# Layer 1 of a two-layer decoder step: squares summed by ScalarE, output halves added by Pool, weight casts on ScalarE

## The chip, the core and the metric

The kernel runs on one core of one Trainium2 chip. A core has five engines with their own instruction queues: TensorE (PE; its weight loads, PEld, overlap its matmuls), VectorE (DVE), ScalarE (ACT), GpSimd (POOL) and SyncE (SP), which here issues every DMA. Each queue runs in order: an instruction that waits holds up all behind it on its engine. The metric is the device time of one execution in microseconds (us), the median of several runs.

## What is computed

One inference step of a two-layer trunk: a prompt of 1024 tokens and 8 groups of 8 sample tokens (64 rows), width 1024. Layer 0 is gated linear attention, layer 1 stick-breaking attention with 16 heads of width 64; the change touches layer 1 alone, and the weight casts of its late part. Cut to layer 1, the reference is:

```python
hp = rms_norm(xp, norm_gain[1]);  u = hp @ w_in_b            # (1024 + 64) x 4096
q = rms_norm(u[..., :1024] by heads of 64, qnorm)
k = rms_norm(u[..., 1024:2048] by heads of 64, knorm)         # k and v are outputs too
v, g = u[..., 2048:3072], u[..., 3072:]
z = q.k / 8 + bias;  valid: key s < query t
rest = reverse cumsum of log(1 - sigmoid(z));  a = exp(z + rest)
x = x + ((a @ v) * silu(g)) @ w_out_b
```

`rms_norm` over a head is x * (mean(x*x) + 1e-6)^-0.5 * gain: for each token and each of its heads a sum of 64 squares.

## The kernel before

Matmuls take two fp32r parts of each operand (a high part and the rest), so each product is three matmuls. Layer 1 goes through 8 pairs of heads. For a pair `p`, `columns` computes q, k and v of each of 8 prompt tiles of 128 tokens and of the sample tile (24 matmuls of 384 columns, `dense`), `gates` the gate of each pair of tiles, and between them stand 20 units of attention, 128 x 512 logits each or a diagonal part of it: `logits` (PE, then two sigmoids `om` and `A` on ACT), `stick` (DVE scans), `turn` (PE transposes, ACT and DVE split the result into `aT`), `weigh` (PE into `po`).

After each tile of q, k, v stands `qk_sums` (L792 to L804): ACT squares the 128 x 256 of q and k from PSUM into `sq`, which has a 65th column per head with the constant 1e-6, and copies v out; DVE sums `sq` by heads into `ms` (L802); POOL raises to -0.5 into `rs` (L804). `qk_scale` (L810) multiplies on DVE from PSUM into `qk`; then the PSUM bank `acc` is free, of which there are two. For every two tiles `qk_p` transposes `qk` on PE and takes it apart with six ACT instructions (`qh` L853, `kc` L854 and L855) and four of DVE (`ql` L856 and L857, `kc` L858 and L859). `sq` has one buffer.

When a pair of heads has finished 256 tokens, `gate_b` joins the two heads: `po` holds the wanted halves on different partitions and columns, so for each half ACT copies one part to `sh` (L952) and DVE adds the other part from PSUM into `og` (L953); POOL multiplies by the gate (L954). This happens 32 times.

The weights are loaded in blocks of 128 x 512; `split` casts a block to the high part (`whi` or `w`), on ACT (L219) if it is used late (`e.first > ACT_FROM`) and `n % 8 < WHI`, else on DVE (L221); POOL subtracts for the low part (L222). Layer 1 from its third pair on, and the output projection, are late: of each 8 blocks 6 go to ACT and 2 to DVE.

Only PE's order is written out by hand, as due times that a heap sorts (`Timeline`, `at`). ACT, DVE, POOL and SP get their order from the framework's own planner. The framework keeps ACT and DVE apart where both would read the same partitions of one PSUM bank.

Of the kernel before, what the change touches and what calls it, by code (L numbers as in the profile page):

```python
# [9 lines left out]
F32 = mybir.dt.float32  # L10
# [3 lines left out]
AF = mybir.ActivationFunctionType  # L14
OP = mybir.AluOpType
AX = mybir.AxisListType
# [11 lines left out]
SH, DH = 16, 64  # L28
# [3 lines left out]
EPS = 1e-6  # L32
# [4 lines left out]
def cut(base, offset, ap):  # L37
    return bass.AP(tensor=base.tensor, offset=base.offset + offset, ap=ap)
# [38 lines left out]
def tile_hybrid_decoder(ctx, tc, x_prompt, x_sample, state_gla, cache_k, cache_v, page_table,  # L77
# [3 lines left out]
    nc = tc.nc  # L81
# [12 lines left out]


    FIRST0, FIRST, FIRST5, RAW0 = 0.9, 1.5, 6, 0.9
    ACT_FROM, WHI, DLO = 90, 6, 3

    GAIN, CONSTS, SUP, LATE = -64.9, 2.5, 0.9, 9
    LAT, LAT0, LQ, LK = .7, 1.2, 1.4, 1.3  # L100
# [18 lines left out]
    def opened(name, side="left", **how):  # L119
        cm = tc.tile_pool(name=name, bufs=2, side=side, reuse_waits="tile", **how)  # L120
        pools[name] = cm.__enter__()
        pools[name, "cm"] = cm
# [5 lines left out]
    def sb(pool, name, shape, dtype=F32, bufs=2, tag=None):  # L128
        return pools[pool].tile(shape, dtype, name=name, tag=tag or name, bufs=bufs)
# [4 lines left out]
    def rows(t):  # L134
        return 128 if t < NP else NS
# [22 lines left out]
    def bcast(dst, src, off, n):  # L158
        nc.sync.dma_start(dst, cut(src, off, [[0, 128], [1, n]]))
# [87 lines left out]
    def rsqrt(dst, mean):  # L247
        nc.gpsimd.tensor_scalar(mean, mean, EPS, None, op0=OP.add)
        nc.gpsimd.tensor_tensor(dst, mean, half_exp[:mean.shape[0], :mean.shape[1]], op=OP.pow)
# [83 lines left out]
    def whole_rows(st, pool, n=512):  # L333
        up = sb(pool, "xr", [128, 512], F32, NX[pool])
        nc.scalar.activation(up[:64, :n], st["ps"][64:128, :n], AF.Copy)
        nc.vector.tensor_add(up[:64, :n], st["ps"][:64, :n], up[:64, :n])
        st["ps"] = up
# [4 lines left out]
    half_exp = const.tile([128, 4], F32, name="half_exp")  # L342
# [73 lines left out]
    for t in range(NP + 1):  # L416
        st = {}
# [14 lines left out]
    for c, (c_0, n) in enumerate(CH):  # L432
        st = {}
# [228 lines left out]
    for h in range(GH):  # L662
# [3 lines left out]
        for c, (c_0, n) in enumerate(CH):  # L666
            st = {}
# [11 lines left out]
            for j, (key, out) in enumerate((("q", q_out), ("k", k_out))):  # L679
                lo, hi = a + (b - a) * 0.5 * j, a + (b - a) * 0.5 * (j + 1)  # L680
                dense_t(lo, hi, c_0, n, wqk,
                        lambda w, k, j=j: (w[k // 2], slice((k % 2) * 256 + j * 128, (k % 2) * 256 + j * 128 + 128)),
# [4 lines left out]
        for t in range(NP + 1):  # L687
            st = {}
# [50 lines left out]
    for c in range(2):  # L739
        w = weights([load_cols(w_out_a, D, k, c * 512, 0, 1, 512) for k in range(NK)])  # L740
        for t in range(NP + 1):
            st = {}
# [24 lines left out]
    K1 = {}  # L767

    def l1_consts():
        opened("keep")  # L770
        opened("at1")
        qn = K1["qn"] = const.tile([128, 1], F32, name="qn")
        for j in range(2):
            nc.sync.dma_start(qn[j * 64:(j + 1) * 64], cut(qnorm_b, 0, [[1, 64], [1, 1]]))
        nc.vector.tensor_scalar(qn, qn, DH ** -0.5, None, op0=OP.mult)
        bcast(K1.setdefault("kn", const.tile([128, DH], F32, name="kn")), knorm_b, 0, DH)
        knt = K1["knt"] = const.tile([128, 1], F32, name="knt")
        for j in range(2):
            nc.sync.dma_start(knt[j * 64:(j + 1) * 64], cut(knorm_b, 0, [[1, 64], [1, 1]]))
        bias = K1["bias"] = const.tile([128, 2, SH], F32, name="bias")  # L780
        bcast(bias[:, 0], sb_bias, 0, SH)
        nc.vector.tensor_scalar(bias[:, 1], bias[:, 0], -1.0, None, op0=OP.mult)
        gains = K1["gains"] = const.tile([128, 1], F32, name="gains")
        nc.vector.tensor_mul(gains, qn, knt)
        for name in ("qTs", "kTs", "gTs"):
            K1[name] = sb("keep", name, [128, PAIRS, NS], F32, 1)

        K1["sq"] = sb("at1", "sq", [128, 4, DH + 1], F32, 1)
        nc.gpsimd.memset(K1["sq"][:, :, DH:], EPS)

    def qk_sums(st, p, t):
        n = rows(t)  # L792
        if t == NP:
            whole_rows(st, "at1", 384)
        ps = st["ps"]
        sq = K1["sq"]
        q4 = ps[:n, :256].rearrange("p (h d) -> p h d", d=DH)
        ms = small.tile([128, 4], F32, name="ms4")
        nc.scalar.activation(sq[:n, :, :DH], q4, AF.Square, scale=1.0 / 8.0)  # L799
        st["v"] = sb("at1", "v", [128, 128])  # L800
        nc.scalar.activation(st["v"][:n], ps[:n, 256:384], AF.Copy)
        nc.vector.tensor_reduce(ms[:n], sq[:n], axis=AX.X, op=OP.add)  # L802
        st["rs"] = small.tile([128, 4], F32, name="rs4")
        nc.gpsimd.tensor_tensor(st["rs"][:n], ms[:n], half_exp[:n], op=OP.pow)  # L804

    def qk_scale(st, p, t):
        n, ps, rs = rows(t), st["ps"], st["rs"]
# [138 lines left out]
    def gate_b(q, pair, p, m):  # L946
        po = q["po"]
        sh, og = sb("at2", "sh", [128, 256], F32, 1), sb("at2", "og", [128, 256], F32, 2)
        q["og"] = og
        for j in range(2):  # L950
            main, other = slice(64 * j, 64 * j + 64), slice(64 - 64 * j, 128 - 64 * j)
            nc.scalar.activation(sh[main], po[other, j], AF.Copy)  # L952
            nc.vector.tensor_add(og[main], po[main, j], sh[main])  # L953
        nc.gpsimd.tensor_mul(og, og, pair["g"][m])  # L954

    def tps(m):
# [13 lines left out]
    def take_h(st, m, g, n):  # L970
        ks = slice(2 * g, 2 * g + n)
        nc.scalar.activation(H[0][:, ks, tps(m)], st[g], AF.Copy)
        nc.vector.tensor_sub(H[1][:, ks, tps(m)], st[g], H[0][:, ks, tps(m)])

    at(i + 0.7, l1_consts)

    def open_at2():
# [12 lines left out]
    for p in range(PAIRS):  # L990
# [4 lines left out]
        def columns(t, i, span):  # L995
            st = {}
            dense(i, t, w, st, span, 384)
            e = i + span
            at(e + 0.02, qk_sums, st, p, t)
            at(e + C_SC, qk_scale, st, p, t)  # L1000
            sts.append(st)
            if t < NP:
                at(max(e + C_SC, open2), v_parts, st, t, pair)
            if t == NP:
                at(e + C_TS, qk_s, st, p)
            elif t % 2 == 1:
                at(max(e + C_T, open2 + 0.01 * t), qk_p, sts[t - 1:], pair)
            at(max(e + C_T, open2) + 0.2, kv_store, st, p, t)
            return e
# [8 lines left out]
        for m in range(NP // 2):  # L1018
            i = columns(2 * m, i, 0.75)
            i = columns(2 * m + 1, i, 0.75)  # L1020
            ready = max(i + UNIT0, open2 + 0.5)
            if m < NP // 2 - 1:
                i = gates(m, i, 0.5)
            else:
                i = gates(m, i, 0.625)
                i = columns(NP, i, 0.5)
            q = {}
            units = [(j, c) for j in range(2) for c in range(m, -1, -1)]
            for x, (j, c) in enumerate(units):
                u = {}  # L1030
                z0 = max(free, ready)
                free = z0 + PACE
                at(z0, logits, u, pair, p, m, c, j)
                at(z0 + L_STICK, stick, u, pair, m, c, j)
                at(z0 + L_TURN, turn, u, m, c)
                at(z0 + L_AV, weigh, u, q, pair, m, c, j, x == 0, x == len(units) - 1)
            at(z0 + L_AV + 0.05, gate_b, q, pair, p, m)
            at(z0 + L_AV + 0.35, store_b, q, p, m)
            if p == PAIRS - 1:
                st = {}  # L1040
                for g in range(4):
                    n = 2 if g < 3 else 1
                    at(i + 0.1 + 0.05 * g, load_h, st, m, g, n)
                    at(i + 0.6 + 0.05 * g, take_h, st, m, g, n)
# [161 lines left out]
    for c, t in steps[:2 * NP - TAIL] + [(0, NP), (1, NP)] + steps[2 * NP - TAIL:]:  # L1206
        if t == NP and c == 0:
            i = max(i, s1 + S_GAP)
        st = {}
# [44 lines left out]
```

## Time and profile before

| | |
|---|---|
| median of 3 runs | 1348.04 us (1348.0 to 1350.47) |
| the profiled execution | 1349.09 us, its span 1347.4 us |
| PE busy | 1269.9 us (94%) |
| DVE busy | 1011.1 us (75%) |
| ACT busy | 708.4 us (53%) |
| POOL busy | 515.5 us (38%) |

The shares are means over the whole span; layer 0, layer 1 and the last projection have different limits. Layer 1's loop over pairs runs from about 524 to 1232 us of the span. A busy PE is not one at its peak: a matmul's listed duration overlaps that of the next. The granted TensorE clock is full throughout.

### The profile page before, as it was taken

To read this page: it belongs to the slowest core of one execution; us is meant where nothing else is said; L and a number is where in the kernel's file an instruction comes from. 1 tells how busy PE (TensorE), PEld (TensorE's weight loads), DVE (VectorE), ACT (ScalarE), POOL (GpSimd) and SP (SyncE) were. 2 spreads that over 40 slices of the span, in tenths; PEclk is the share of its full clock that TensorE was granted. 3 is DMA by queue.
4 is the path that set the end of the run, shared out by engine and by line. 5 is a ranking of instruction groups with operands and counts; after the bars stand their busy time and mean duration, and the time that the engine had idled before them with its cause. 6 is when DMAs were issued, how large, how long until landed. Compare 5 with 4: busy or idle time off the path is not lost.

```text
span 1347.4 us, 23358 instructions
## 1 busy us (share of the span) xinstructions
PE 1269.9 (94%) x8025; PEld 1128.5 (84%) x8025; DVE 1011.1 (75%) x2047; ACT 708.4 (53%) x1640; POOL 515.5 (38%) x847
## 2 busy tenths in 40 slices
PE   6899999999999999989989999899998999999998
PEld 5788888888887787889989899898898998978665
DVE  7857858759565357698898988988889889896543
ACT  6446245254352034566666766667667677763221
POOL 6222323223222215363453734646446464443000
PEclk9999999999999999999999999999999999999999
DMA  6311402403327443020120200202002022134862
GB/s 193 91 41 44 135 20 59 124 17 100 121 90 240 135 137 117 20 73 27 34 71 23 71 27 28 79 23 70 28 28 77 21 78 86 33 124 152 316 204 79
DMA packets 118456, 115.80 MB, mean 86 GB/s; under 512 B 11002, under 2 KB 97922, under 8 KB 118338
## 3 DMA queue, kind: packets, MB, share of 16 engines
q1 hardware_dynamic: 118338, 114.31, 27.5%
q8 instruction: 64, 1.05, 0.3%
q14 instruction: 54, 0.44, 0.1%
HBM read 83.61 MB, written 30.67 MB: 85 GB/s over the span
## 4 chain that ended last, share of the span: by engine, by line
PE 56%; DVE 25%; ACT 7%; issue 5%; POOL 4%; DMA 3%; SPq 0%; DVEq 0%; POOLq 0%; ACTq 0%
PE acc L293 33%; PE acc L315 6%; DVE run L907 4%; PE z L881 3%; PE tr L928 3%; PE o L942 2%; DVE aT L931 2%; DVE whi L221 2%; ACT qh L853 2%; DVE qk L810 1%; POOL rs L804 1%; DVE A L912 1%; DVE A L915 1%; PE o L544 1%; DVE run L904 1%
## 5 line engine op out<-in xcount | busy, mean ns | idle before, releaser
L293 PE MATMUL acc<-whi,h 128*128 128x512 f32 (+1 forms) x1728 | 538.1, 374 | 9.3 <-DVE qk L810 6.2
L293 PEld LDWEIGHTS acc<-whi,h 128*128 128x128 f32 x1728 | 312.8, 189 | 40.3 <-ACT sh L952 3.8
L293 PE MATMUL acc<-wlo,h 128*128 128x512 f32 (+1 forms) x864 | 322.6, 373 | 3.9 <-DVE wlo L222 2.5
L315 PE MATMUL acc<-h,whi 128*128 128x256 f32 (+5 forms) x832 | 191.7, 316 | 19.1 <-DVE qk L810 8.7
L222 POOL TENSOR_TENSOR wlo<-wr,whi 128x512 fp32r<-128x512 f32 x98 | 144.4, 1478 | 127.4 <-DVE whi L221 92.5
L293 PEld LDWEIGHTS acc<-wlo,h 128*128 128x128 f32 x864 | 162.5, 188 | 22.1 <-DVE wlo L222 3.2
L315 PEld LDWEIGHTS acc<-h,whi 128*128 128x128 f32 (+2 forms) x832 | 137.8, 185 | 26.2 <-issue 10.6
L907 DVE TENSOR_TENSOR_SCAN run<-om,run 128x256 f32<-128x256 f32 x192 | 141.8, 779 | 15.6 <-ACT om L884 15.1
L930 ACT ACTIVATE aT<-tr 128x512 fp32r<-128x512 f32 (+1 forms) x160 | 89.0, 556 | 82.8 <-PE tr L928 80.9
L884 ACT ACTIVATE om<-z,bias 128x512 f32<-128x512 f32 (+1 forms) x160 | 103.1, 644 | 48.3 <-PE z L881 39.6
L293 PE MATMUL acc<-w,h 128*128 128x384 f32 (+1 forms) x480 | 122.0, 365 | 0.8 <-DVE qk L810 0.8
L315 PE MATMUL acc<-h,wlo 128*128 128x256 f32 (+2 forms) x392 | 122.2, 312 | 0.3 <-POOL wlo L222 0.3
L931 DVE TENSOR_TENSOR aT<-tr,aT 128x512 fp32r<-128x512 f32 (+1 forms) x160 | 100.9, 631 | 9.7 <-ACT aT L930 7.4
L928 PE MATMUL tr<-ident,A 128*128 128x128 f32 x576 | 90.0, 274 | 18.6 <-DVE kc L859 8.4
L885 ACT ACTIVATE A<-z,bias 128x512 f32<-128x512 f32 (+1 forms) x160 | 102.4, 640 | 0.0
L942 PE MATMUL o<-aT,v 128*128 128x256 f32 (+1 forms) x640 | 98.1, 274 | 0.0
L928 PEld LDWEIGHTS tr<-ident,A 128*128 128x128 f32 x576 | 68.9, 140 | 34.0 <-ACT sq L799 9.0
L942 PEld LDWEIGHTS o<-aT,v 128*128 128x128 f32 x640 | 94.4, 188 | 1.7 <-DVE aT L931 1.0
L804 POOL TENSOR_TENSOR rs<-ms,half_exp 128x4 f32<-128x4 f32 (+1 forms) x72 | 86.2, 1198 | 21.3 <-DVE ms L802 18.8
L881 PE MATMUL z<-kc,qh 128*128 128x256 f32 x320 | 84.4, 286 | 7.2 <-DVE kc L858 7.2
L293 PEld LDWEIGHTS acc<-w,h 128*128 128x128 f32 x480 | 83.2, 189 | 6.3 <-issue 0.8
L899 POOL COPY run<-run 128x2 f32<-128x2 f32 x96 | 32.8, 342 | 135.7 <-DVE run L907 78.1
(273 smaller groups left out, 2488.7 us busy)
## 6 DMA issues: line engine op xcount, KB each, us to landing
wr<-in_w_in_b_dram SPq DMA_DIRECT2D x64, 256.0 KB, 3.0
wr<-in_w_in_a_dram SPq DMA_DIRECT2D x32, 256.0 KB, 2.9
kp<-in_cache_k_dram SPq DMA_DIRECT2D x16, 512.0 KB, 4.6
vp<-in_cache_v_dram SPq DMA_DIRECT2D x16, 512.0 KB, 4.9
o_d<-og SPq DMA_DIRECT2D x60, 128.0 KB, 1.8
x<-in_x_prompt_dram SPq DMA_DIRECT2D x8, 512.0 KB, 5.2
wr<-in_w_in_a_dram SPq DMA_DIRECT2D x32, 128.0 KB, 3.9
n<-in_state_gla_dram SPq DMA_DIRECT2D x8, 512.0 KB, 4.2
```

Of the source, the lines that this page charges most:

```text
L222: engine.tensor_sub(e.lo[:, :m], raw[:, :m], e.hi[:, :m])
L293: nc.tensor.matmul(st["ps"][:x.shape[1], :n], x, (w[k].hi if part == 0 else w[k].lo)[:, :n], start=first, stop=last)
L315: nc.tensor.matmul(st[key][:x.shape[1], :n], x, y, start=first, stop=last)
L804: nc.gpsimd.tensor_tensor(st["rs"][:n], ms[:n], half_exp[:n], op=OP.pow)
L881: nc.tensor.matmul(out, lhs, rhs, start=x == 0, stop=x == len(mm) - 1)
L884: nc.scalar.activation(u["om"][:, v0:], z[:, v0:], AF.Sigmoid, scale=-1.0, bias=K1["bias"][:, 1, hd:hd + 1])
L885: nc.scalar.activation(u["A"][:, v0:], z[:, v0:], AF.Sigmoid, bias=K1["bias"][:, 0, hd:hd + 1])
L907: nc.vector.tensor_tensor_scan(run[:, a, n - 1::-1], rev, rev, before[:, a, 0:1], op0=OP.mult, op1=OP.bypass)
L928: nc.tensor.transpose(tr[:, x], u["A"][:, col:col + 128], ident)
L930: nc.scalar.activation(hi[:, v0:], tr[:, v0:], AF.Copy)
L931: nc.vector.tensor_sub(lo[:, v0:], tr[:, v0:], hi[:, v0:])
L942: nc.tensor.matmul(q["po"][:, j, q0:], vs, part[:, x * 256 + q0:(x + 1) * 256], start=first and n == 0, stop=last and n == 3)
```

## The change

Three edits, all in layer 1 but for four blocks of the output projection's weights:

- `qk_sums`: in place of one square over 256 columns, four squares over 64 columns each, every one of which also writes its sum by ScalarE's accumulator; the sum on DVE and the constant column go, and POOL adds 1e-6 ahead of the power (`rsqrt`, two POOL instructions in place of one).
- `gate_b`: ACT copies both parts of each half (four copies in place of two), and one add on POOL over 128 x 256 takes the place of two adds on DVE over 64 x 256.
- `WHI` from 6 to 8: every late weight cast is on ACT.

```diff
-    ACT_FROM, WHI, DLO = 90, 6, 3
+    ACT_FROM, WHI, DLO = 90, 8, 3
...
-        K1["sq"] = sb("at1", "sq", [128, 4, DH + 1], F32, 1)
-        nc.gpsimd.memset(K1["sq"][:, :, DH:], EPS)
+        K1["sq"] = sb("at1", "sq", [128, 4, DH], F32, 1)
...
-        nc.scalar.activation(sq[:n, :, :DH], q4, AF.Square, scale=1.0 / 8.0)
+        for h in range(4):
+            nc.scalar.activation(sq[:n, h], q4[:, h], AF.Square, scale=1.0 / 8.0, accum_out=ms[:n, h:h + 1])
         st["v"] = sb("at1", "v", [128, 128])
         nc.scalar.activation(st["v"][:n], ps[:n, 256:384], AF.Copy)
-        nc.vector.tensor_reduce(ms[:n], sq[:n], axis=AX.X, op=OP.add)
         st["rs"] = small.tile([128, 4], F32, name="rs4")
-        nc.gpsimd.tensor_tensor(st["rs"][:n], ms[:n], half_exp[:n], op=OP.pow)
+        rsqrt(st["rs"][:n], ms[:n])
...
             main, other = slice(64 * j, 64 * j + 64), slice(64 - 64 * j, 128 - 64 * j)
+            nc.scalar.activation(og[main], po[main, j], AF.Copy)
             nc.scalar.activation(sh[main], po[other, j], AF.Copy)
-            nc.vector.tensor_add(og[main], po[main, j], sh[main])
+        nc.gpsimd.tensor_add(og, og, sh)
         nc.gpsimd.tensor_mul(og, og, pair["g"][m])
```

`rsqrt`, which layer 0 already uses (L248, L249), is:

```python
    def rsqrt(dst, mean):
        nc.gpsimd.tensor_scalar(mean, mean, EPS, None, op0=OP.add)
        nc.gpsimd.tensor_tensor(dst, mean, half_exp[:mean.shape[0], :mean.shape[1]], op=OP.pow)
```

## Rows read from the trace of the kernel before

**Rows 1.** Busy time by stretch: start:end, length, then each engine's busy us (instructions).

```profile
524.00:1232.00 708.00, 662.36 (x4550) 627.82 (x4549) 605.44 (x1159) 468.85 (x996) 351.53 (x595) 1.00 0.18 53
752.00:776.00 24.00, 20.77 (x139) 19.08 (x138) 23.58 (x38) 17.45 (x37) 20.43 (x23) 1.00 0.32 92
```

**Rows 2.** The page's chain that ended last, whole span, by engine.

```profile
PE 56%; DVE 25%; ACT 7%; issue 5%; POOL 4%; DMA 3%; SPq 0%; DVEq 0%; POOLq 0%; ACTq 0%
```

**Rows 3.** PE's waits, 524 to 1232 us: total us, times, longest.

```profile
PE acc L315 <- DVE qk L810: 10.4, 7, 1.7
PE tr L928 <- DVE kc L859: 8.4, 6, 2.4
PE z L881 <- DVE kc L858: 7.2, 10, 1.4
PE acc L293 <- DVE qk L810: 7.0, 14, 1.2
PE tr L928 <- ACT sq L799: 4.5, 7, 1.0
```

**Rows 4.** ACT's waits, 524 to 1232 us, same columns.

```profile
ACT qh L853 <- PE tr L829: 19.9, 24, 2.6
ACT sq L799 <- DVE ms L802: 6.6, 7, 1.3
```

**Rows 5.** Timelines of ACT, DVE, POOL, PE around one tile: start, us, engine, line, tiles.

```profile
773.57 0.38 ACT L799 ACTIVATE sq<-acc 128x256 f32<-128x256 f32 x1 [0.74 <-PE acc L293]
...
777.74 0.42 DVE L802 TENSOR_REDUCE ms<-sq 128x4 f32<-128x260 f32 x1
...
778.24 1.01 POOL L804 TENSOR_TENSOR rs<-ms,half_exp 128x4 f32<-128x4 f32 x1
...
779.28 0.42 DVE L810 TENSOR_TENSOR qk<-acc,rs 128x256 f32<-128x256 f32 x1 [0.66 <-POOL rs L804]
...
779.85 0.41 PE L293 MATMUL acc<-w,h 128*128 128x384 f32 x1 [0.24 <-DVE qk L810]
```

**Rows 6.** Groups by line (L221: 590 to 1260 us): count, busy us, mean ns, idle before.

```profile
L802 DVE TENSOR_REDUCE ms<-sq 128x4 f32<-128x260 f32 (+1 forms) x72 | 29.1, 405 | 0.9 <-ACT sq L799 0.9
L953 DVE TENSOR_TENSOR og<-o,sh 64x256 f32<-64x256 f32 x64 | 26.6, 415 | 2.8 <-ACT sh L952 1.1
L221 DVE CAST whi<-wr 128x512 fp32r<-128x512 f32 x11 | 7.6, 693 | 0.0
L221 DVE CAST w<-wr 128x512 fp32r<-128x512 f32 x5 | 3.2, 631 | 2.0 <-DMA wr<-in_w_out_b_dram 2.0
```

**Rows 7.** ACT's timeline in layer 0: a square with accumulator, and what follows it.

```profile
202.59 0.39 ACT L645 ACTIVATE og<-o 128x256 f32<-128x256 f32 x1
202.87 0.20 ACT L645 ACTIVATION_READ_ACCUMULATOR og<-o 128x1 f32 x1
202.96 0.38 ACT L529 ACTIVATE gt<-acc 128x256 f32<-128x256 f32 x1
```

**Rows 8.** Groups by line, 524 to 1232 us: nearest rows of the added work.

```profile
L866 ACT ACTIVATE gTs<-acc 128x64 f32<-128x64 f32 x8 | 1.7, 218 | 0.0
L952 ACT ACTIVATE sh<-o 64x256 f32<-64x256 f32 x64 | 24.3, 379 | 39.5 <-DVE og L953 35.4 <-PE o L942 3.1
L219 ACT ACTIVATE whi<-wr 128x512 fp32r<-128x512 f32 x36 | 22.4, 631 | 6.0 <-DMA wr<-in_w_in_b_dram 5.6 <-DMA wr<-in_w_out_b_dram 0.3
L954 POOL TENSOR_TENSOR og<-og,gt 128x256 f32<-128x256 f32 x32 | 26.6, 830 | 37.9 <-DVE og L953 37.9
```

**Rows 9.** Line L248, layer 0's add ahead of the power: ns min/median/max.

```profile
L248 POOL TENSOR_SCALAR ms<-ms x36: 216/224/557, 75.7 to 417.1; 128x1 f32<-128x1 f32 x32, 64x1 f32<-64x1 f32 x4
```

**Rows 10.** DVE's timeline: the same two scans beside POOL's L954 and without it.

```profile
752.51 1.83 DVE L907 TENSOR_TENSOR_SCAN run<-om,run 128x256 f32<-128x256 f32 x2
...
775.62 1.38 DVE L907 TENSOR_TENSOR_SCAN run<-om,run 128x256 f32<-128x256 f32 x2
```

**Rows 11.** POOL's timeline beside the first of them.

```profile
752.56 1.24 POOL L954 TENSOR_TENSOR og<-og,gt 128x256 f32<-128x256 f32 x1
```

## The prediction

> **What bounds the kernel now.** I read the busy times by stretch first, because the shares of the whole span mix layers and the change touches layer 1 alone. There [rows 1] PE is busy 662 of 708 us, DVE 605 (86%), ACT 469 (66%), POOL 352 (50%). So PE comes first and DVE is close behind it; over the middle 24 us of one pair of heads DVE is busy for 23.6, while PE falls to 20.8 and ACT to 17.5. In that stretch DVE sets the pace, in the rest of the pair PE does. The chain that ended last says the same of the whole span [rows 2]: PE 56%, DVE 25%, ACT 7%, POOL 4%. What can be won is therefore PE's idle time in layer 1, and the next view is who ends it [rows 3]. Two families hold most of it: PE waits for a bank of `acc`, which `qk` on DVE sets free (10.4 + 7.0 = 17.4 us), and for `kc` on DVE, the end of a burst of six ACT and four DVE instructions after the transposes of `qk` (8.4 + 7.2 = 15.6 us, 16 waits); 4.5 us are marked with the square on ACT, that is, with how far ACT's queue has come. The last view is ACT's own waits, because ACT receives the work: it stands 35.4 us before the second `sh`, held by DVE's first add [rows 8], and 6.6 us before the square, held by the sum in the single `sq` [rows 4]. During these 42 us nothing behind gets out of ACT's queue.
>
> **What DVE loses.** 72 sums of 0.405 us (29.1 us), 64 adds (26.6 us) and the 16 casts still on DVE from the third pair on (7.6 + 3.2 = 10.8 us) [rows 6]: 66.5 of its 605 us. Little of DVE's work is left over as idle time, so nearly all of it moves DVE's queue forward; on PE's waits only a part shows.
>
> **What ACT gains.** No row of layer 1 shows an accumulating square, but layer 0 has one [rows 7]: the square runs 0.39 us, the read of the accumulator starts 0.28 us after it, and the next instruction 0.09 us after that. So a read costs a slot of 0.09 us and a square gives up its slot about 0.11 us before its listed end. The nearest 64-column instruction from PSUM lasts 0.218 us [rows 8], a slot of 0.11. Four heads take 4 x (0.11 + 0.09) = 0.80 us against 0.28 now: +0.52 us, by 72 tiles +37 us. The other end is that nothing overlaps: 4 x (0.218 + 0.20) = 1.67 against 0.39, +1.28 us a tile, +92 us. I take the first, since the overlap is read from the very pair of instructions; the second is a rival. The 64 further copies are like `sh`, 0.379 us listed, 0.28 as slots: +18 us (at most 24). The casts are 16 x 0.63 us = 10 us [rows 8]. Together +65 us (at most +126). Against it the 42 us of standing still fall away: `sq` is no longer read by anybody, and the copies of `po` need no DVE between them. ACT is thus bound for 469 + 65 = 534 us (75%), at most 595 (84%).
>
> The Trainium skill ("ScalarE: Activation LUTs", What ACT_TABLE_LOAD costs) gives 186 ns plus 0.833 ns an element for such an instruction, and 93 ns of overlap back to back. That would make 64 columns 239 ns, where the row has 218; as an estimate from the page four squares would take 4 x 146 = 584 ns of slots, without the reads, for which it has no price.
>
> **What POOL gains.** 72 adds of 1e-6, 0.224 us for one column [rows 9] and hardly more for four: 16 us; no lower than zero, no higher than 0.3 us each, since the instruction is nearly all fixed cost. And 32 adds over 128 x 256 like the multiply beside them, 0.830 us [rows 8]: 27 us. POOL goes from 352 to 395 us (56%). Both stand in chains: the first between the squares and `rs`, the second ahead of the gate multiply, which only a store waits for. Behind them in POOL's queue stand the copies of `run`, for which DVE's multiply waits, and the low parts of weights.
>
> POOL's add also takes something from DVE. Two scans that take 1.38 us alone took 1.83 us beside POOL's multiply of the same shape, which itself took 1.24 us [rows 10, 11]. Thirty-two adds cost DVE 32 x 0.45 = 14 us by that; nothing if they fall beside other work, 32 x 1.24 = 40 us if DVE stood still throughout. I take 14 us, from the row of the same shape. Net DVE loses 66.5 - 14 = 52 us.
>
> **The sum, on PE's waits.**
> 1. The `acc` bank, 17.4 us. In the tile shown [rows 5] the square ended at 773.95, DVE came to the sum at 777.74, `rs` ran to 779.25 and `qk` followed. After the change the squares would end by 774.5, the add and the power by 776, and `qk` could follow the scans two us earlier. Elsewhere the way is one of 0.5 us through DVE, which the longer squares and the added POOL instruction give back. I take half: -9 us, with ends of -17 and 0.
> 2. The burst before `kc`, 15.6 us. ACT's part begins after a wait for PE's transposes 24 times in 32 [rows 4], and there nothing in front of it matters. The other 8 may have a set of squares in front: 8 x 0.52 = +4 us, ends -3 (DVE comes earlier to its part) and 8 x 1.28 = +10.
> 3. What is left of DVE's relief, 26.6 + 10.8 - 14 = 23 us, shortens the end only where DVE is on the chain, 25% [rows 2]: -6 us, ends -23 and 0.
> 4. ACT's net load, 65 - 42 = +23 us, at its 7% of the chain [rows 2]: +2 us, ends -4 (the waits marked with the square) and +6 (84 x 7%).
>
> Together -9 us. From the profiled execution's 1349.1 us (span 1347.4 and 1.7 around it) that is 1340; the median lies 1 us lower, so 1339 us. Layer 0 and the last projection keep their work but for four casts.
>
> **Rivals.**
> *No change.* PE's order is fixed by hand and the power on POOL stays in the chain; if `rs` then ends the same waits a little later (add 0.22 us, squares 0.52 us, against a sum of 0.42 us taken out), steps 1 and 3 give nothing that step 2 doesn't take: 1348 us. For it: `qk` already waited for `rs` in the tile shown [rows 5]. Against it: the 3.8 us before the sum there.
>
> *Slower, ACT ends last.* The accumulator lets nothing overlap, a set of squares holds ACT for 1.67 us, and in the sigmoids' and `aT`'s way. ACT then is bound for 84% of layer 1, as DVE is now. Of the 72 sets a third, about what DVE and ACT hold of the chain together [rows 2], stands in front of something that PE waits for: 24 x 1.28 = +31 us. The same third of the 42 us of standing still is won, -14 us; steps 1 and 3 give nothing, since ACT is late instead of DVE: 1348 + 31 - 14 = 1365 us. It decides from the point where a set costs more than the standing still that it ends, 42 us / 72 = 0.58 us a tile; my 0.52 is close below, and that is the weakest point of the forecast.
>
> *Slower, Pool's port.* If DVE stands still through POOL's whole add, 40 us are lost against the 26.6 saved, and the gate's chain is an instruction longer. At 25% to 50% on the chain that is +3 to +7 us, with step 1 lost 1352 to 1356. The Trainium skill says so ("GPSIMD Engine Reference", Engine selection): elementwise work with two inputs belongs on VectorE, GpSimd being about twice as slow. By the rows the engine time is a draw here: one add of 0.830 us [rows 8] for two of 0.415 over half the partitions each [rows 6].
>
> **How the numbers follow.** Forecast (1322 to 1345) 50%, no change 17%, ACT last 22%, Pool's port 11%. This kernel's measurement can tell about 0.2%, 2.7 us, from no change. So faster 0.50, same 0.17, slower 0.33. Cases of both signs are open, so the range goes from 1322 (steps 1 and 3 near their ends, -26 us) to 1364, just short of the whole of the ACT rival: that leaves out some 15 of the 22% and the far end of the forecast.
>
> **What would show it.** In the profile after: an ACT line of 288 short squares and as many reads, and the start of one to the next tells 0.20 us from 0.42; PE's waits for `qk` down from 17.4 to under 10 us; ACT's waits for `og` and `ms` gone; DVE's busy time in layer 1 at 540 to 555 us. PE's waits for `kc` above 26 us, or ACT above 80% in layer 1, would speak for the ACT rival; scans longer on the mean than now, for the Pool rival. The forecast is wrong if the planner puts the four squares in front of the sigmoids.

## The result, and the profile after

The changed kernel takes 1363.69 us (median of 4 runs, 1361.17 to 1364.02), the kernel before 1348.02 in the same session: a ratio of 1.0106, 95% interval [1.0093, 1.0119]. It is slower by 1.1%, where 1339 us was forecast. The result lies inside the stated range only because its end of 1364 was set by the rival with ACT, which didn't come true (below). The profiled execution took 1361.17 us, with a span of 1358.7.

The busy times of layer 1 in the kernel after, columns as in [rows 1]:

```profile
524.00:1232.00 708.00, 657.64 (x4494) 623.70 (x4493) 567.95 (x1004) 529.70 (x1572) 400.94 (x697) 1.00 0.17 52
```

The engine loads came out near the forecast: DVE 568 us (forecast 553), ACT 530 (534), POOL 401 (395). PE, the engine that matters, did 5 us less work in the same stretch than before [rows 1]. Who it waited for (total us, times, longest; compare [rows 3]):

```profile
PE acc L315 <- DVE qk L808: 18.8, 8, 2.9
PE acc L293 <- DVE qk L808: 7.9, 14, 1.2
PE z L879 <- ACT sq L798: 4.7, 8, 0.9
PE tr L926 <- ACT sq L798: 4.0, 7, 0.6
PE tr L926 <- DVE A L913: 3.9, 7, 1.0
```

The waits for `kc`, 15.6 us before, have all but gone (3.2 us in all, below these rows). The waits for `qk` went from 17.4 to 26.7 us. ACT's own longest waits name neither `og` nor `ms` any more, so what was to fall away there did:

```profile
ACT aT L928 <- PE tr L926: 71.2, 71, 3.4
ACT om L882 <- PE z L879: 35.9, 70, 2.0
ACT qh L851 <- PE tr L827: 24.1, 18, 6.1
```

And the squares overlap as forecast. ACT's timeline around one set:

```profile
775.05 0.22 ACT L798 ACTIVATE sq<-acc 128x64 f32<-128x64 f32 x1
775.16 0.21 ACT L798 ACTIVATION_READ_ACCUMULATOR sq<-acc 128x1 f32 x1
775.25 0.28 ACT L800 ACTIVATE v<-acc 128x128 f32<-128x128 f32 x1
```

The four squares of this set start at 774.47, 774.66, 774.86 and 775.05 and `v` follows at 775.25: 0.195 us a head with its read, 0.78 us a set, where 0.80 was forecast and 1.67 was the rival's.

So what was slow? Follow the set just shown through POOL, DVE and PE. It belongs to the first tile of a pair of heads (POOL's, DVE's and PE's rows in turn):

```profile
775.97 1.28 POOL L222 TENSOR_TENSOR wlo<-wr,whi 128x512 fp32r<-128x512 f32 x1
777.33 0.29 POOL L248 TENSOR_SCALAR ms<-ms 128x4 f32<-128x4 f32 x1
777.68 0.52 POOL L817 CAST v<-v 128x128 fp32r<-128x128 f32 x1
778.18 0.56 POOL L810 TENSOR_TENSOR kout<-qk,kn 64x128 f32<-64x128 f32 x1
778.70 1.41 POOL L249 TENSOR_TENSOR rs<-ms,half_exp 128x4 f32<-128x4 f32 x1
780.09 1.25 POOL L222 TENSOR_TENSOR w<-wr,w 128x512 fp32r<-128x512 f32 x1
...
779.21 2.43 DVE L910 TENSOR_TENSOR A<-A,run 128x128 f32<-128x128 f32 x2
781.55 0.68 DVE L929 TENSOR_TENSOR aT<-tr,aT 128x512 fp32r<-128x512 f32 x1
782.15 0.41 DVE L808 TENSOR_TENSOR qk<-acc,rs 128x256 f32<-128x256 f32 x1
...
782.71 0.95 PE L315 MATMUL acc<-h,w 128*128 128x256 f32 x6 [2.87 <-DVE qk L808]
```

The sums are there at 775.4. POOL comes to the add at 777.33, then does a cast of `v` and a `kout`, and comes to the power 1.37 us after the add had begun. `rs` is there at 780.11, but DVE's list has products with `run` and an `aT` in front of `qk`, which starts 2.04 us later. PE stands 2.87 us. From the end of the squares to `qk` are 6.88 us. In the kernel before the same tile needed 6.96 us, and PE stood 1.72 for it:

```profile
775.25 0.96 PE L315 MATMUL acc<-h,w 128*128 128x256 f32 x6 [1.72 <-DVE qk L810]
```

The chain that the change was to shorten is as long as it was, only filled with other things, and PE comes to it sooner: its last matmul ahead of the wait ends 4.57 us after the squares, where it was 5.80. In the matmuls ahead of it in this pair a wait of 1.20 us for `A` on ACT is down to 0.15. Over layer 1 PE gains 12.4 us at `kc` and loses 9.3 at `qk`.

Most of the 2.04 us from `rs` to `qk` is not the length of DVE's list. Of the two products `A` in front of `qk` the second, over 256 columns, takes 2.24 us, where the same product takes 0.42 us with no POOL work beside it; POOL's low part of a weight runs beside it from 780.09 to 781.34. It is so in six of the eight pairs, and was so before (1.90 us). POOL's work beside DVE thus has a share in the way to `qk`.

A second place is the start of layer 1, where 3.5 us are lost in 14 (POOL, DVE, PE):

```profile
531.44 0.57 POOL L248 TENSOR_SCALAR ms<-ms 128x4 f32<-128x4 f32 x1
532.07 0.29 POOL L817 CAST v<-v 128x128 fp32r<-128x128 f32 x1
532.30 0.18 POOL L894 MEMSET run<- 128x1 f32 x4
532.44 3.07 POOL L222 TENSOR_TENSOR w<-wr,w 128x512 fp32r<-128x512 f32 x2
535.47 0.46 POOL L818 TENSOR_TENSOR v<-v,v 128x128 fp32r<-128x128 f32 x1
535.88 1.04 POOL L249 TENSOR_TENSOR rs<-ms,half_exp 128x4 f32<-128x4 f32 x1
...
533.02 1.35 DVE L286 CAST h<-hs 128x256 fp32r<-128x256 f32 x1
534.29 0.41 DVE L866 TENSOR_TENSOR gt<-gt,acc 128x256 f32<-128x256 f32 x1
536.96 0.43 DVE L808 TENSOR_TENSOR qk<-acc,rs 128x256 f32<-128x256 f32 x1 [2.26 <-POOL rs L249]
...
534.76 0.44 PE L293 MATMUL acc<-whi,h 128*128 128x384 f32 x1 [1.92 <-DVE gt L866]
```

From the start of the add to the power are 4.4 us here, with two low parts of weights among what lies between. In the kernel before, this tile's power ran at 529.42 and its `qk` at 532.03. But PE doesn't stand for this `qk`. It stands 1.92 us for `gt`, which DVE reaches late, behind a cast of `h` that takes 1.35 us beside POOL's low parts (0.28 at 531.89, without them); the rest of the loss is the lower clock behind it. Without the 1e-6 PE stands 2.61 us at the same place, so this wait isn't the added instruction's, as theory 1 below takes it to be.

Over all 72 tiles the planner puts something between the add and the power in 49; the cast of `v` is there each time.

### The profile page after: what moved, and what is told of

Same layout as the page of the kernel before. It is cut to its first block, busy times and chain, and to the rows that moved or that the text cites. A ratio compares the mean times of both kernels' runs of the same rounds, so it can differ in the third digit from the quotient of the medians.

```text
span 1358.7 us, 23861 instructions
## 1 busy us (share of the span) xinstructions
PE 1274.9 (94%) x8025; PEld 1132.4 (83%) x8025; DVE 977.2 (72%) x1895; ACT 773.3 (57%) x2224; POOL 565.5 (42%) x950
## 5 line engine op out<-in xcount | busy, mean ns | idle before, releaser
L293 PE MATMUL acc<-whi,h 128*128 128x512 f32 (+1 forms) x1728 | 539.5, 375 | 11.3 <-DVE qk L808 6.8
L222 POOL TENSOR_TENSOR wlo<-wr,whi 128x512 fp32r<-128x512 f32 x98 | 138.3, 1416 | 128.4 <-DVE whi L221 85.5
L905 DVE TENSOR_TENSOR_SCAN run<-om,run 128x256 f32<-128x256 f32 x192 | 147.9, 810 | 21.0 <-ACT om L882 20.0
L248 POOL TENSOR_SCALAR ms<-ms 128x4 f32<-128x4 f32 (+3 forms) x108 | 34.9, 323 | 234.8 <-ACT og L645 126.1
L249 POOL TENSOR_TENSOR rs<-ms,half_exp 128x4 f32<-128x4 f32 (+3 forms) x108 | 106.8, 989 | 4.9
```

The source lines that it names most:

```text
L222: engine.tensor_sub(e.lo[:, :m], raw[:, :m], e.hi[:, :m])
L293: nc.tensor.matmul(st["ps"][:x.shape[1], :n], x, (w[k].hi if part == 0 else w[k].lo)[:, :n], start=first, stop=last)
L905: nc.vector.tensor_tensor_scan(run[:, a, n - 1::-1], rev, rev, before[:, a, 0:1], op0=OP.mult, op1=OP.bypass)
```

## The experiments

All were timed in five rounds beside the kernel before (1348.7 to 1349.1 us). The theories, as the expectations number them: 1 (and 1b) says that the forecast's gains are there and that the 1e-6, now an instruction of its own on POOL, eats them, because it lengthens the chain square, power, `qk`; 2 is that ACT ends last; 3 is that POOL's adds of the outputs hold up DVE. Where an expectation names a theory, it says again what it means there.

The table's last columns are worked out from each kernel's trace: the sum of all of PE's waits from 520 to 1300 us and those for `qk` in them, the time that PE spent at the lower clock there (from windows of 2 us, by the granted clock), and the time from the end of a tile's squares to its `qk`, as the mean of the 72 tiles and for the tile followed above.

| kernel | median us | ratio to before, 95% | PE's waits | for `qk` | lower clock | squares to `qk`, mean | that tile |
|---|---|---|---|---|---|---|---|
| before | 1348.0 | | 48.0 | 17.4 | 0 | 4.03 | 6.96 |
| after | 1363.7 | 1.0093 to 1.0119 | 52.2 | 26.7 | 6.8 | 3.60 | 6.88 |
| squares alone (`e_squares`) | 1377.0 | 1.0196 to 1.0224 | 62.0 | 30.6 | 27.3 | 3.79 | 8.52 |
| gate alone (`e_gate`) | 1350.1 | 1.0004 to 1.0024 | 48.5 | 14.1 | 3.4 | 4.06 | 6.94 |
| casts alone (`e_casts`) | 1343.9 | 0.9959 to 0.9977 | 39.6 | 18.0 | 3.4 | 3.88 | 6.21 |
| after, no 1e-6 (`e_noadd`) | 1340.1 | 0.9925 to 0.9952 | 39.7 | 4.5 | 0 | 2.48 | 3.22 |
| the same, idle add (`e_dummy`) | 1345.0 | 0.9956 to 0.9983 | 41.9 | 2.5 | 13.6 | 2.50 | 3.31 |
| the same, no gate edit (`e_nogate`) | 1344.9 | 0.9949 to 0.9974 | 41.9 | 5.5 | 6.8 | 2.43 | 3.06 |
| after, `v` cast held in place (`e_pinned`) | 1353.7 | 1.0019 to 1.0043 | 47.0 | 13.7 | 10.2 | 3.02 | 5.65 |
| after, add on ACT (`e_actadd`) | 1383.1 | 1.0244 to 1.0283 | 65.8 | 45.7 | 40.9 | 4.12 | 8.56 |
| after, add on DVE (`e_dveadd`) | 1351.3 | 1.0009 to 1.0029 | 42.2 | 17.7 | 10.2 | 3.51 | 6.15 |
| before, plus the add (`b_add`) | 1388.0 | 1.0274 to 1.0305 | 71.6 | 44.4 | 34.1 | 4.72 | 9.93 |
| squares alone, no 1e-6 (`e_squares_noadd`) | 1355.2 | 1.0034 to 1.0061 | 53.7 | 5.5 | 3.4 | 2.70 | 4.67 |
| gate and casts (`e_gate_casts`) | 1343.7 | 0.9951 to 0.9978 | 39.0 | 14.4 | 10.2 | 3.95 | 6.39 |

PE's waits plus half of the time at the lower clock explain most of the differences in span: `b_add` 23.6 + 17 = 41 us for 38.9 measured, `e_squares` 14 + 14 = 28 for 27.9, `e_noadd` -8.3 for -10.3; of after's 11.3 us they cover 4.2 + 3.4. `e_actadd` (38 for 33) and `e_dummy` (0.7 for -4.1) fit worst.

**Each edit alone.** First the squares, then the gate, then the casts, each in the kernel before:

```diff
-        nc.scalar.activation(sq[:n, :, :DH], q4, AF.Square, scale=1.0 / 8.0)
+        for h in range(4):
+            nc.scalar.activation(sq[:n, h], q4[:, h], AF.Square, scale=1.0 / 8.0, accum_out=ms[:n, h:h + 1])
...
-        nc.vector.tensor_reduce(ms[:n], sq[:n], axis=AX.X, op=OP.add)
-        nc.gpsimd.tensor_tensor(st["rs"][:n], ms[:n], half_exp[:n], op=OP.pow)
+        rsqrt(st["rs"][:n], ms[:n])
```

> The kernel before with the first edit alone: four accumulating squares per tile on ACT, DVE's sum gone, add and power as two POOL instructions. Theory 1 (the power has become two POOL instructions, and the planner puts other POOL work between them: before the second tile of layer 1 two weight low parts of 3.07 us together): this edit carries most of the loss, 1355 to 1361 us, with layer 1's first lump of 3.5 us in it. Theory 2 (ACT's added time, whichever edit brings it): about half of the loss, 1352 to 1357 us. Theory 3 (POOL's adds of the outputs hold up DVE): no loss here, 1346 to 1350 us.

```diff
+            nc.scalar.activation(og[main], po[main, j], AF.Copy)
             nc.scalar.activation(sh[main], po[other, j], AF.Copy)
-            nc.vector.tensor_add(og[main], po[main, j], sh[main])
+        nc.gpsimd.tensor_add(og, og, sh)
```

> The kernel before with the second edit alone: four ACT copies and one POOL add in place of two ACT copies and two DVE adds. Theory 1: nearly nothing, 1346 to 1351 us. Theory 2: 18 to 24 us of the about 65 us added on ACT less the standing still that ends, so 1347 to 1352 us. Theory 3: most of the loss, 1355 to 1361 us, and longer scans on DVE.

```diff
-    ACT_FROM, WHI, DLO = 90, 6, 3
+    ACT_FROM, WHI, DLO = 90, 8, 3
```

> The kernel before with the third edit alone: the 16 late casts that DVE had go to ACT. Theories 1 and 3: no difference that can be measured, 1346 to 1350 us. Theory 2: 10 us more on ACT, where the stretch with the casts is the fullest of a pair, 1349 to 1353 us.

The squares alone cost 28 us, more than the whole change and than any of the theories had; the gate costs about 2; the casts gain 4 to 5, which no theory had. So the loss sits in the first edit, and the other two soften it: the mean way from squares to `qk` is 3.79 us with the squares alone and 3.60 with all three. The Trainium skill ("GPSIMD Engine Reference", Engine selection) would have the gate's addition stay on VectorE; alone the edit costs 0.14%, beside the casts nothing (1343.7 against 1343.9), beside squares and casts, without the 1e-6, it gains 4.8 us (1344.9 without it, 1340.1 with it). For the 1344.9 (`e_nogate`) I had named 1343 to 1348 us if the end of ACT's standing still is worth something, 1339 to 1342 if the edit is neutral and 1330 to 1337 if POOL's adds hold up DVE; it is the first. The runs bear the rule out only where DVE's other work stays.

**The 1e-6 left out.** The power reads the accumulated sums directly:

```diff
-        rsqrt(st["rs"][:n], ms[:n])
+        nc.gpsimd.tensor_tensor(st["rs"][:n], ms[:n], half_exp[:n], op=OP.pow)
```

> The changed kernel with the power as one POOL instruction; the 1e-6 is left out of the mean of squares in layer 1's heads. Theory 1: the first lump of 3.5 us, the falls of the clock behind PE's long waits, and part of the first pair's loss go: 1347 to 1353 us. Theory 2: ACT has the same work, so as the changed kernel, 1360 to 1365 us. Theory 3: the same, 1359 to 1364 us.

1340.1 us: below the 1347 to 1353 that theory 1 had, and the forecast's number, with every other part of the change in place. The number agrees better than its terms: against before, PE's waits for `qk` fell by 12.9 us and those for `kc` by 12.4, where 9 less and 4 more were forecast, and those for the product `A` on DVE rose by 11.3 and those marked with the square by 6. 23.6 us hang on an instruction that lasts 0.35 us on the mean. PE's longest waits in this kernel:

```profile
PE tr L926 <- DVE A L910: 9.9, 6, 1.7
PE tr L926 <- ACT sq L798: 5.3, 8, 1.5
PE z L879 <- ACT sq L798: 5.2, 8, 1.5
PE acc L293 <- DVE qk L808: 4.5, 7, 0.7
```

The waits for `qk` fell from 17.4 to 4.5 us. The same tile as above, in POOL and DVE (its squares ended at 766.2):

```profile
766.58 1.68 POOL L222 TENSOR_TENSOR wlo<-wr,whi 128x512 fp32r<-128x512 f32 x1
768.22 1.19 POOL L802 TENSOR_TENSOR rs<-ms,half_exp 128x4 f32<-128x4 f32 x1
769.37 0.29 POOL L817 CAST v<-v 128x128 fp32r<-128x128 f32 x1
769.62 0.45 POOL L810 TENSOR_TENSOR kout<-qk,kn 64x128 f32<-64x128 f32 x1
...
769.45 0.42 DVE L808 TENSOR_TENSOR qk<-acc,rs 128x256 f32<-128x256 f32 x1 [0.31 <-POOL rs L802]
769.79 2.68 DVE L902 TENSOR_TENSOR_SCAN run<-om,eye 128x128 f32<-128x128 f32 x2
```

The cast and `kout` now come behind the power, and `qk` stands ahead of DVE's scans, not behind them: 3.22 us instead of 6.88. PE doesn't wait at all at this place. A few matmuls on it stands 1.65 us, for the product behind those scans, one of which is now the instruction held beside POOL's low part (1.88 us): so part of the gain goes back, in the 9.9 us at `A` above. This kernel has all of ACT's added work and the gate's adds on POOL, and is the fastest of all: theories 2 and 3 fall.

**The same POOL time, off the chain.** `e_noadd` plus an add of the same form into a tile that nobody reads any more:

```diff
+        nc.gpsimd.tensor_scalar(gain[:n, :4], ms[:n], EPS, None, op0=OP.add)
```

> As e_noadd (the power is one POOL instruction, the 1e-6 is left out of the mean of squares in layer 1's heads), and behind the power an add of the same form on POOL, out of ms into a spare tile that nobody reads. So POOL has the changed kernel's work, but nothing stands between squares and power. Theory 1a (POOL's time: one instruction of some 0.3 us more per tile in a queue that is full where the weights are split): most of the 23.6 us between e_noadd and the changed kernel come back, 1355 to 1363 us. Theory 1b (the chain squares, power, qk has got longer by the add and by what the planner puts between add and power): 1340 to 1346 us.

1345.0 us, 4.9 more than without. The way from squares to `qk` is all but unchanged (2.50 us for 2.48), so POOL's time as such costs at most about a fifth of the 23.6 us; and as this execution spent 13.6 us more at the lower clock, it is not even clear that POOL's time is the cause. The rest is the add's place in the chain.

**The cast of `v` kept from between add and power.** Its place in the order is held as written:

```diff
-        nc.gpsimd.tensor_copy(v4[:, 0::3], v2)
+        tc.keep_in_program_order(nc.gpsimd.tensor_copy(v4[:, 0::3], v2))
```

> The changed kernel, with POOL's cast of v held behind what was issued before it on POOL, so that it no longer stands between add and power: in the planned order 63 of 72 tiles have the power right behind the add, in place of 23. Theory 1b with the interposed work as the larger part: 1345 to 1354 us. Theory 1b with the add itself as the larger part, or theory 1a: 1357 to 1364 us. Either way the start of layer 1 keeps its lump, since the two weight low parts stay between add and power of the second tile.

1353.7 us. Add and power are now neighbours in 63 tiles instead of 23, the mean way falls from 3.60 to 3.02 us and the waits for `qk` from 26.7 to 13.7. Ten of the 23.6 us come back by order alone, nothing being left out. Thirteen stay: in seven of the eight pairs `kout` still stands between in the first tile, and in the tile followed above `qk` still comes 1.32 us after its `rs`, with three of DVE's scans and products put in front of it. In the kernel after these are five, two scans, two products and an `aT`; without the 1e-6 there are none. The product among the three takes 1.71 us beside POOL's low part, where such a one over 128 columns takes 0.26 alone; that is about the 1.5 us that PE still stands there in six of the pairs.

**The add on another engine.** On ACT, and on DVE:

```diff
-        rsqrt(st["rs"][:n], ms[:n])
+        nc.scalar.activation(ms[:n], ms[:n], AF.Copy, bias=EPS)
+        nc.gpsimd.tensor_tensor(st["rs"][:n], ms[:n], half_exp[:n], op=OP.pow)
```

> The changed kernel with the 1e-6 added on ACT, behind the four squares, in place of POOL; all the computation is there. The chain keeps an instruction more, but in a queue where nothing long can come between. Theory 1b with the interposed work as the larger part: 1341 to 1347 us. Theory 1b with the length of the chain as such: 1350 to 1360 us. Theory 1a: 1340 to 1346 us. Theory 2 (ACT's added time): 1364 us or more, since ACT gets 72 instructions more than in the changed kernel.

```diff
-        rsqrt(st["rs"][:n], ms[:n])
+        nc.vector.tensor_scalar(ms[:n], ms[:n], EPS, None, op0=OP.add)
+        nc.gpsimd.tensor_tensor(st["rs"][:n], ms[:n], half_exp[:n], op=OP.pow)
```

> The whole change, with the 1e-6 added by DVE instead of POOL, so that POOL has the power alone; nothing is left out. Theory 1b in its general form (any added step between squares and power waits for its engine's queue, whichever engine it is): slower than the 1340.1 us without the add, 1348 to 1375 us, as DVE's queue is the fullest of the three. Rival (it is POOL's own time and queue that made the add dear): 1338 to 1346 us, PE's waits for qk under 8 us.

On ACT I had expected it to be cheap; it is the dearest place for it, 1383.1 us. Only theory 2 had such a number, but the waits for `qk` hold 45.7 of PE's 65.8 us, and those marked with the square, 4.3, are no more than before. In the tile followed above the squares end at 781.2 and the power begins at 788.2: the add waits in ACT's list behind `v`, `aT`, a cast and the two activations for `om` and `A` until 783.2, and the power then behind POOL's other work, another tile's power among it. On DVE it takes 1351.3 us, 11 more than without, although DVE's list is the fullest. So the price isn't the step's own time but the place that the planner finds for it. Among the nine kernels with accumulating squares the waits for `qk` grow with the mean way, whichever engine the step is on: 2.5 to 5.5 us at a way of 2.4 to 2.7, 13.7 at 3.02, 17.7 at 3.51, 26.7 at 3.60, 30.6 at 3.79, 45.7 at 4.12. The kernels with the sum on DVE lie on another line (17.4 at 4.03), so the way alone doesn't tell across the two.

**The squares as in the change, without the 1e-6.** `e_squares` and the diff of `e_noadd` together:

> The first edit alone, with the 1e-6 left out (the power follows the squares directly); the gate and the casts as before. The first edit alone with the add took 1377.0 us. Theory 1b: the add costs here as much as in the whole change or more (23.6 us), so 1343 to 1354 us, PE's waits for qk under 10 us. Rival (the squares on ACT themselves hold the chain up, and only the other two edits make room for them): 1360 us or more, waits for qk above 20 us.

1355.2 us: 21.8 less than with the add, so the add costs here what it costs in the whole change, as expected. The 6.5 us over before that remain are just above the range. There the waits for `qk` are down to 5.5 us, and those marked with `aT`, `A` and the square are up. The accumulating squares pay only beside both other edits and without the 1e-6: 1340.1 us against 1343.7 for gate and casts without them. Beside the casts alone they don't (1344.9 against 1343.9).

**The add alone.** In the kernel before, with the sums still on DVE, only the 1e-6 moves from the 65th column to POOL (`sq` has 64 columns a head, as in the change; that part of the diff isn't shown):

```diff
-        nc.scalar.activation(sq[:n, :, :DH], q4, AF.Square, scale=1.0 / 8.0)
+        nc.scalar.activation(sq[:n], q4, AF.Square, scale=1.0 / 8.0)
...
-        nc.gpsimd.tensor_tensor(st["rs"][:n], ms[:n], half_exp[:n], op=OP.pow)
+        rsqrt(st["rs"][:n], ms[:n])
```

> The kernel before with only the place of the 1e-6 changed: the square writes 64 columns a head, DVE sums 64 instead of 65, and the 1e-6 is added by POOL's own instruction ahead of the power. Everything else is as before. Theory 1b (the added POOL instruction stands in the chain square, sum, power, qk, and the planner puts other work around it): 1358 to 1372 us, PE's waits for qk up from 17.4 to 24 us or more. Rival (the add costs much only together with the squares on ACT, which bring the sums sooner): 1348 to 1354 us, waits for qk within 4 us of before's 17.4.

1388.0 us, 39 more than before and well above my upper end of 1372. POOL and PE around the followed tile, whose squares ended at 780.33:

```profile
784.28 0.48 POOL L248 TENSOR_SCALAR ms<-ms 128x4 f32<-128x4 f32 x1
784.84 0.45 POOL L811 TENSOR_TENSOR kout<-qk,kn 64x128 f32<-64x128 f32 x1
785.25 1.28 POOL L222 TENSOR_TENSOR w<-wr,w 128x512 fp32r<-128x512 f32 x1
787.15 0.19 POOL L898 COPY run<-run 128x2 f32<-128x2 f32 x1 [0.61 <-DVE run L903]
787.29 0.64 POOL L819 TENSOR_TENSOR v<-v,v 128x128 fp32r<-128x128 f32 x1
787.89 1.03 POOL L249 TENSOR_TENSOR rs<-ms,half_exp 128x4 f32<-128x4 f32 x1
...
790.82 1.62 PE L315 MATMUL acc<-h,w 128*128 128x256 f32 x6 [4.45 <-DVE qk L809]
```

Four instructions stand between add and power, one of which waits for a scan on DVE, which has nothing to do with this tile. 9.93 us from squares to `qk`, and PE stands 4.45. It happens in the first tile of six of the eight pairs. The lower clock, told at the end, adds up to 17 us.

**Gate and casts without the squares.** Two diffs from above.

> The second and third edit together, without the first; nothing is left out. If the edits add up: 1348.0 + 2.1 - 5.1 (their own differences from the median before, taken alone) = 1345, range 1342 to 1348. If the gate edit is worth 5 us beside the casts, as it was between the two kernels without the 1e-6 (1344.9 and 1340.1): 1336 to 1341.

1343.7 us, as if the edits added up; the waits for `qk` stay at 14.4. With `e_casts` (1343.9) it is the fastest kernel here that computes everything, 0.3% under before.

## Why the prediction was wrong

The step that failed is the first of the sum, the `acc` bank: -9 us with ends of -17 and 0, measured +9.3 (26.7 us after). What it says of the squares and of DVE's sum was sound: without the 1e-6 the waits went down by 12.9 us, inside the ends. What was mis-sized is the term "72 adds of 1e-6, no lower than zero, no higher than 0.3 us each". It was priced as POOL's time, from a duration (0.224 us [rows 9]), and in the step it was set directly ahead of the power ("the add and the power by 776"). It lasts 0.35 us on the mean beside other work, 25 us in all; but over the 72 tiles the way from squares to `qk` is 80.6 us longer with it (3.60 against 2.48 us each), three times its duration. The rest is what the planner puts around one more step of the chain: other work between add and power, and a `qk` that loses its place in front of DVE's scans and products, of which one is drawn out by POOL's low part of a weight. So the far end of that step should have stood above zero. [rows 5] showed in the kernel before that POOL's power came late and `qk` right behind it; I didn't ask which work was queued beside them and could slip in. Nor was the way elsewhere "one of 0.5 us through DVE": in the kernel before the sum began 1.54 us after the end of the square on the mean of the 72 tiles, and about 0.5 us after it in 23 of them.

That tile was also not where the gain lay. Without the 1e-6 its way from squares to `qk` goes only from 5.33 to 5.05 us; the gain is in the tile before it, 6.96 to 3.22.

The other steps. The burst before `kc` (15.6 us, forecast +4) fell by 12.4 us. The forecast had the wrong sign: the casts alone take it to 8.8, the squares alone to 8.7, the gate alone to 9.7, squares and casts (`e_nogate`) to 2.6. DVE's part of the burst, for which I had allowed 3 us at the far end, came earlier: in the last burst of a pair it began 1.5 to 2.8 us after ACT's last `kc` before, and 0.1 us after it now in seven of the eight pairs. How this splits was not opened further. DVE's relief (-6) can't be told from this. ACT's net load (+2) shows as waits marked with the square, 8.7 us for 4.5, so +4; ACT's busy time, the slot of a square and the end of ACT's waits for `og` and `ms` were right.

The Trainium skill ("ScalarE: Activation LUTs", What ACT_TABLE_LOAD costs) leads to 239 ns for 64 columns; the squares took 224 at the median, and with its read a head takes a slot of 195 ns, where the estimate from the page was 146 without one. It changed nothing.

Of the rivals, the one with ACT gave 1365 us and the result is 1363.7, but the agreement is in the number only: ACT stood at 75%, not 84, a set cost 0.78 us, not 1.67, and `e_noadd` has the same ACT work at 1340. The rival with Pool's port fell as it was put, on the gate's adds: the same scans took 811 ns on the mean against 779, 6 us in all where 14 were forecast, and `e_noadd` has 798. What holds DVE up in front of `qk` is POOL's low parts, which were there before. The rival "no change" had named the right place, `rs` and the power on POOL, but at 0.22 us for the add; no rival had it with the work that comes in between. Nor had the sum anything for the lower clock.

What stays open: of the 21.6 us between the two profiled spans (1358.7 and 1337.1), 12.5 are PE's waits and up to 3.4 the lower clock; the remaining six or so are in none of the rows I read. No run moves POOL's low parts away from `qk`, so what they cost by themselves is not shown. Whether a planner told to keep add and power together in every tile, and `qk` right behind, would reach 1340 was not tried.

## What to carry over

A small instruction added to a chain that crosses engines costs not only its duration but another wait in a queue, with whatever the scheduler puts in front of it and of everything behind it; price it from the work queued on that engine at that place, and give the price an end on the losing side. Where a constant can ride along in work that is done anyway, as the 65th column did here, removing it isn't free. And look what another engine runs beside the instructions that come in front: here POOL drew out DVE's. Before moving work, try the added step by itself in the old kernel: `b_add` would have told the sign at once.

## What the runs showed of the hardware

A long wait of PE can be paid twice. In the kernel before, the granted clock stands at 1.00 throughout layer 1. In `b_add` it falls to half, that is 1.2 GHz instead of 2.4, during the 4.45 us of waiting shown above, and the matmuls behind it run at that (the third column from the right):

```profile
784.00:790.00 6.00, 2.21 (x13) 1.62 (x11) 5.87 (x10) 1.87 (x5) 4.50 (x8) 1.00 0.37 104
790.00:791.00 1.00, 0.18 (x1) 0.21 (x2) 1.00 (x3) 0.00 (x0) 0.86 (x3) 0.58 0.00 0
791.00:794.00 3.00, 3.00 (x15) 3.00 (x16) 0.14 (x1) 0.49 (x1) 1.89 (x4) 0.50 0.08 22
```

Over layer 1 this kernel spends 34.1 us at the lower clock, which is up to 17 of its 39 us. In the kernel after it happens twice in layer 1, 6.8 us in all, the first time behind the wait at its start (1.92 us, `gt`). A stall of PE in this kernel can thus have a price that its own row doesn't show. Its length alone doesn't tell: of six waits of 2.85 to 2.91 us in the kernel after, five were not followed by the lower clock, nor was one of 2.61 us in `e_noadd`.

POOL's low parts of weights (128 x 512) draw out DVE's scans and products of two operands in SBUF, and leave instructions that take one of them from PSUM alone. From 524 to 1232 us of the kernel after, the product `A` over 256 columns takes 0.42 us with no POOL work beside it and 1.26 us on the mean beside a low part, 2.24 at most; `aT` over 512 columns, which reads PSUM, takes 0.69 and 0.68 us.

The accumulator's read costs ACT 0.09 us of its time behind a short square as behind a long one: it is listed with 0.21 us, but all but that overlaps.
